# Three pairs of gate/up chunks in a SwiGLU feed-forward layer computed with tokens stationary and 512 weight columns moving

## The chip, the cores and the metric

The kernel runs on one core of a Trainium2 chip. The metric is the device time of one execution in microseconds (us). Five engines work side by side, each with its own instruction stream: TensorE (PE, with its weight loads as PEld), VectorE (DVE), ScalarE (ACT), GpSimd (POOL) and SyncE (SP, which here only issues DMAs). They wait for each other on semaphores. [...]

## What is computed

One layer of a hybrid encoder: three token mixers, a merge, an output projection, then a SwiGLU feed-forward part. The change is in the feed-forward part, with 512 tokens, D_MODEL = 1024 and D_FF = 2816, all in float32:

```
h2 = rms_norm(x, norm_ffn[l])
act = jax.nn.silu(jnp.einsum('bsd,df->bsf', h2, w_ffn_gate[l])) * jnp.einsum('bsd,df->bsf', h2, w_ffn_up[l])
x = x + jnp.einsum('bsf,fd->bsd', act, w_ffn_down[l])
```

## The kernel before

**Precision.** TensorE's fast float32 format (fp32r) keeps fewer bits than float32. So each operand is split into a high part (an ACT copy into fp32r) and a low part (a DVE subtraction, operand minus high part), and each product of blocks takes three matmuls: high by high, high by low, low by high. Weights are loaded by DMA as float32 and split on the chip, which costs one ACT and one DVE instruction per 128x1024 weight tile.

**Seven products for eight.** The 2816 columns of the gate and the up weight are taken in 11 chunks of 256. Chunks 0 and 1 are "direct" (`chan_chunk`, 128x512 matmuls). Chunks 2 to 10 use a 2x2 scheme of Strassen and Winograd (`seven`, L1543): the inner dimension 1024, the 512 tokens and the 256 columns are each halved, and of the eight block products only seven are computed, with sums of weight blocks (S1 to S4, `sums_a`, L1488, four DVE additions of 128x1024 per chunk) and differences of token blocks (T1 to T4, `diff_b`, L1454, computed once). Their order is `ORDER`: 11, 12, S2, S1, S3, S4, 22. A weight tile holds the block of the gate and that of the up weight side by side (128 partitions x 2 x 4 x 128).

**One product** (`product`, L310) is 24 matmuls: 128 weight columns are stationary, 256 token columns move, over 2 weights x 4 steps of the inner dimension x 3 parts. The result lies with channels on the partitions, as the down projection needs it. Partial results are copied out of PSUM by ACT (L1562) and the rest is added by DVE (L1536); `finish_act` (L1533) then applies Silu on ACT (L1537) and multiplies on DVE (L1538).

**Order of the work.** `make_a` (L1495) stays three products ahead of TensorE: it makes sums and splits (`split_a`, L1505: ACT at L1508, DVE at L1509) into tiles of three buffers. `load_a` (L1482) loads a chunk with eight SP DMAs of 256 KB, into a pool of eight tiles ("cor") one chunk ahead; the same eight tiles first hold the normalised tokens and T1 to T4 while `prepare_b` (L1458) splits them (DVE at L1451, sums at L1456). So a tile for weights comes free when DVE has read the token block in it. SP takes its DMAs strictly in order, so one whose tile is not free holds back all behind it. The order on each engine is otherwise set by a scheduler that follows the program's order. PSUM has four tiles of two banks ("mm", the pool `fp`).

**Elsewhere in the kernel** there are two stages of a form that the prediction needs. The q, k and v projections (L800 to L870) already use seven products with 128x512 matmuls (L844), an ACT copy (L857), a DVE addition (L865), a DVE transpose (L814), a store to DRAM by POOL and a load back. The down projection (L1602 to L1756) gets sums of its weights by accumulating POOL DMAs (L1629) onto tiles that SP loaded (L1626, L1641).

Of the kernel before, what the change touches and what calls it, by code (L numbers as in the profile page):

```python
# [16 lines left out]
P = 128  # L17
S = 512
D = 1024
# [3 lines left out]
NF = DFF // P  # L23
# [4 lines left out]
WARM = 9  # L28
GBUFS = 27
NDIRECT = 2  # L30
KD = 10
NTICK = (1, 1)
H = S // 2
# [29 lines left out]

@with_exitstack
def layer_kernel(ctx: ExitStack, tc: tile.TileContext, x, xt, vecs, w_in, w_qkv7, w_gate7, w_pool, w_rg, w_ig,
                 w_branch, w_br7, w_out, w_fg, w_fu, w_fd, w_fd7, out):
    nc = tc.nc
    act = nc.scalar.activation
    dve = nc.vector
# [3 lines left out]
    wp = ctx.enter_context(tc.tile_pool(name="wp", bufs=3))  # L73
# [4 lines left out]
    dr = ctx.enter_context(tc.tile_pool(name="dr", bufs=1, space=bass.MemoryType.DRAM))  # L78
# [12 lines left out]
    def cols(ap, k0, nk, c0, nc_):  # L91
        return ap[k0 * P:(k0 + nk) * P, c0:c0 + nc_].rearrange("(k p) c -> p k c", p=P)
# [217 lines left out]
    def product(a_, b_, ps, half, first, last, ws=(0, 1)):  # L310
        for w in ws:
            o = ps[:, w, half * H:(half + 1) * H]
            for k in range(4):
                for n, (a, b) in enumerate(((0, 0), (0, 1), (1, 0))):
                    nc.tensor.matmul(o, a_[a][:, w, k, :], il2(b_[b][:, k, :]),  # L315
                                     start=first and n == k == 0,
                                     stop=last and n == 2 and k == 3, skip_group_check=True)
# [119 lines left out]
    with ExitStack() as first:  # L437
# [411 lines left out]
        for t in VKQ:  # L849
            ps = {}  # L850
# [120 lines left out]
    with ExitStack() as mix:  # L971
# [299 lines left out]
        def corner(shape, name, dt=F32):  # L1271

            return cor.tile([P] + shape, dt, tag="r", name=name)
# [19 lines left out]
    with ExitStack() as third:  # L1293
# [42 lines left out]
        for u, nm in BORDER:  # L1336
# [5 lines left out]
            b = BH[nm]  # L1342
# [22 lines left out]
    with ExitStack() as ffn:  # L1365
# [85 lines left out]
            dve.tensor_tensor(l, BN[key], h.bitcast(F32), ALU.subtract)  # L1451
            B[which, nm] = h, l

        def diff_b(nm, x, y):  # L1454
            BN[nm] = corner([4, H], f"hn{nm}")
            dve.tensor_tensor(BN[nm], BN[x], BN[y], ALU.subtract)  # L1456

        def prepare_b():  # L1458
            nrm = [lambda k=k: norm2(k) for k in range(8)]
            return nrm[:4] + [lambda: split_b("11", (0, 0))] + nrm[4:] + [  # L1460
                lambda: split_b("21", (1, 0)),
                lambda: diff_b("T1", (0, 1), (0, 0)),
                lambda: diff_b("T2", (1, 1), "T1"),
                lambda: split_b("T2", "T2"),
                lambda: split_b("T1", "T1"),
                lambda: diff_b("T3", (1, 1), (0, 1)),
                lambda: split_b("T3", "T3"),
                lambda: split_b("22", (1, 1)),
                lambda: diff_b("T4", (1, 0), "T2"),
                lambda: split_b("T4", "T4")]  # L1470

        SUMS = {"S2": (("S3", "11", "21", ALU.subtract), ("S2", "22", "S3", ALU.subtract)),
                "S1": (("S1", "21", "22", ALU.add),),
                "S4": (("S4", "12", "S2", ALU.subtract),)}
# [5 lines left out]
        made = [0, NDIRECT]  # L1480

        def load_a(c):  # L1482
            for nm in ("11", "21", "22", "12"):
                raw[c, nm] = t = corner([2, 4, P], f"w{c}_{nm}")
                for w in range(2):
                    nc.sync.dma_start(t[:, w], cols((w_fg, w_fu)[w], KH[nm] * 4, 4, c * 256 + CH[nm] * P, P))

        def sums_a(c, nm):  # L1488
            for s_, x, y, op in SUMS.get(nm, ()):
                if (c, s_) in raw:  # L1490
                    continue
                raw[c, s_] = t = wp.tile([P, 2, 4, P], F32, tag="raw", name=f"w{c}_{s_}")
                dve.tensor_tensor(t, raw[c, x], raw[c, y], op)

        def make_a(upto):  # L1495
            while made[0] < min(upto, len(steps)):
                c, nm = steps[made[0]]
                made[0] += 1
                while made[1] < min(c + 2, DOWN):
                    load_a(made[1])  # L1500
                    made[1] += 1
                sums_a(c, nm)
                A[c, nm] = split_a(raw[c, nm], f"{c}_{nm}")

        def split_a(src, n):  # L1505
            h, l = (t.rearrange("p (w k c) -> p w k c", w=2, k=4)
                    for t in weight_tiles("wh" + n, "wl" + n))
            act(h, src, AF.Copy)  # L1508
            dve.tensor_tensor(l, src, h.bitcast(F32), ALU.subtract)  # L1509
            return h, l  # L1510

        acts = []
        DB = {}


# [17 lines left out]
        def finish_act(t, ps, a):  # L1533

            v = two2(t)
            dve.tensor_tensor(v, v, in_order2(ps), ALU.add)  # L1536
            act(t[:, 0, :], t[:, 0, :], AF.Silu)  # L1537
            dve.tensor_tensor(a, t[:, 0, :], t[:, 1, :], ALU.mult)  # L1538


        PRE = ("S2", "S1", "S3")
# [1 line left out]
        def seven(c):  # L1543
            a = g4([2, S], f"act{c}")
            tx, ty = g4([2, S], f"tx{c}"), g4([2, S], f"ty{c}")
            Y = fp.tile([P, 2, S], F32, tag="mm", name=f"ps_y{c}")
            X = fp.tile([P, 2, S], F32, tag="mm", name=f"ps_x{c}")
            lo, hi = slice(0, H), slice(H, S)
            plan = (("11", Y, 1, True, tx, lo, Y, hi),
                    ("12", X, 0, True, None, None, None, None),  # L1550
                    ("S2", Y, 1, False, tx, hi, Y, hi),
                    ("S1", X, 1, False, ty, hi, X, hi),
                    ("S3", Y, 1, False, ty, lo, Y, hi),
                    ("S4", X, 1, False, None, None, None, None),
                    ("22", Y, 0, False, None, None, None, None))
            n0 = steps.index((c, "11"))
            for n, (nm, ps, half, first, t, ts_, src, ss) in enumerate(plan):
                with tc.issue_after(last) if (c, n) == (NDIRECT, 3) else nullcontext():
                    make_a(n0 + n + 3)
                product(A.pop((c, nm)), B[0, WITH[nm]], ps, half, first, True)  # L1560
                if t is not None:
                    last = act(two2(t[:, :, ts_]), in_order2(src[:, :, ss]), AF.Copy).ins  # L1562
                if c == DOWN - 1 and nm in PRE:
                    split_d2("11", PRE.index(nm), 0, 0)
                if nm == "S4":
                    finish_act(tx, X, a[:, 0, :])
                if nm == "22":
                    finish_act(ty, Y, a[:, 1, :])
                if (c, n) in after:
                    after[c, n]()  # L1570
            acts.append(a)

        bg.extend([lambda: None, rms2] + prepare_b())
        for c in range(NDIRECT):
            pg = chan_chunk(("fg", c), h2, 3, fp)
            pu = chan_chunk(("fu", c), h2, 3, fp)
            if c == NDIRECT - 1:
                make_a(3)
            a = g4([2, S], f"act{c}")

            def direct_act(j, c=c, a=a, pg=pg, pu=pu):
                sg = small(f"sg{c}{j}", 2, "sq2")
                dve.tensor_tensor(two(sg), in_order(pg[j]), two(rb2), ALU.mult)
# [6 lines left out]
            acts.append(a)  # L1590
        tick(len(bg))
        after = {(NDIRECT, 1): lambda: direct_act(0), (NDIRECT, 2): lambda: direct_act(1)}
# [164 lines left out]


_INS = ["x", "xt", "vecs", "w_in", "w_qkv7", "w_gate7", "w_pool", "w_rg", "w_ig", "w_branch", "w_br7", "w_out",
        "w_ffn_gate", "w_ffn_up", "w_ffn_down", "w_down7"]  # L1760


# [41 lines left out]
```

## Time and profile before

| what | value |
|---|---|
| three timed runs | 859.97, 858.64, 859.10 us, median 859.1 |
| profiled execution, its own time | 858.89 us |
| its span in the trace | 856.8 us |
| direct gate/up matmuls end, chunk 2 begins | 580.5 us |
| chunks 2 to 7 | 580.5 to 693.2 us |
| chunks 8 to 10 | 693.2 to 749.5 us |

All positions are from the start of the span; 2.1 us lie around it. In the rows of the profile, `L315 PE` is an operation of TensorE issued at line 315, `out<-in` names the tiles, `xN` counts instructions, then come the busy time in us and the mean of one in ns, and behind the second bar the idle time of the engine ahead of them with what ended it. A DVE instruction's duration overlaps the next one's start by some 0.08 us, so a row's mean is a little longer than the distance between two starts.

### The profile page before, as it was taken

The page shows a single profiled execution, that of the slowest core. Times are in us where ns is not written, and L with a number is a line of the kernel's source. Part 1 is how long each engine was busy: PE and PEld are TensorE (multiplying, and loading weights), DVE is VectorE, ACT ScalarE, POOL GpSimd, SP SyncE. Part 2 cuts the span into 40 slices and gives each one's busy share as a digit, 9 for nine tenths or more (in the row PEclk, how much of TensorE's full clock was granted, in tenths as well). Part 3 has the DMA queues.
Part 4 walks back from the last instruction along what each step waited for, and adds up shares of the span by engine and source line. Part 5 has one row for each costly group of instructions (what it writes and reads, how often), then busy time and mean ns, then how long its engine had stood idle before and what let it go on. Part 6 is the DMA issues. An engine that isn't in the chain of part 4 may idle for free.

```text
span 856.8 us, 14307 instructions
## 1 busy us (share of the span) xinstructions
PE 850.3 (99%) x5483; PEld 781.2 (91%) x5483; DVE 732.3 (85%) x937; ACT 533.3 (62%) x863; POOL 88.6 (10%) x128
## 2 busy tenths in 40 slices
PE   9999999999999999999999999999999999999998
PEld 7888888888889988889889988889999999999998
DVE  7899898987897699967997877799988888999974
ACT  6554999658887657556665544455655555755642
POOL 1110002123324102000001100000000000121200
PEclk9999999999999999999999999999999999999999
DMA  9586356798585768846668854364533434797913
GB/s 343 160 286 205 101 167 200 215 316 262 141 257 129 228 170 239 246 116 171 174 204 212 182 197 148 99 164 136 145 99 109 114 101 142 221 238 204 199 32 123
DMA packets 141988, 154.09 MB, mean 180 GB/s; under 512 B 41696, under 2 KB 115424, under 8 KB 141920
## 3 DMA queue, kind: packets, MB, share of 16 engines
q1 hardware_dynamic: 129248, 107.30, 40.6%
q0 software_dynamic: 12528, 45.62, 22.5%
q8 instruction: 43, 0.70, 0.3%
q10 hardware_dynamic: 144, 0.26, 0.1%
q14 instruction: 25, 0.20, 0.1%
HBM read 132.71 MB, written 18.87 MB: 177 GB/s over the span
## 4 chain that ended last, share of the span: by engine, by line
PE 88%; ACT 4%; DVE 4%; issue 3%; POOL 1%; DMA 0%; DVEq 0%; POOLq 0%
PE ps_y L315 11%; PE ps_x L315 8%; PE ps_dy L1723 6%; PE ps_q L844 5%; PE ps_dx L1723 5%; PE ps_br L306 3%; PE ps_br L307 3%; PE ps_br L308 3%; PE ps_bY L1347 3%; PE ps_gy L315 3%; PE ps_gate L736 2%; PE ps_bX L1347 2%; PE ps_gx L315 2%; PE ps_pool L308 2%; PE ps_pool L306 2%
## 5 line engine op out<-in xcount | busy, mean ns | idle before, releaser
L141 ACT ACTIVATE whi<-raw 128x1024 fp32r<-128x1024 f32 x69 | 72.9, 1056 | 75.6 <-PE ps_br L307 18.4
L142 DVE TENSOR_TENSOR wlo<-raw,whi 128x1024 fp32r<-128x1024 f32 x69 | 84.2, 1220 | 22.4 <-ACT whi L141 21.9
L142 DVE TENSOR_TENSOR wlo<-qw,whi 128x1024 fp32r<-128x1024 f32 x48 | 58.3, 1220 | 11.6 <-ACT whi L141 11.2
L141 ACT ACTIVATE whi<-qw 128x1024 fp32r<-128x1024 f32 x48 | 50.4, 1052 | 23.6 <-PE ps_q L844 12.8
L1508 ACT ACTIVATE wh_S<-w_S 128x1024 fp32r<-128x1024 f32 x36 | 38.3, 1063 | 28.7 <-PE ps_y L315 20.0
L1629 POOL DMA_DIRECT2D dw<-in_w_down_dram x20 | 17.0, 855 | 305.3 <-DMA dw<-in_w_down_dram 247.7
L1509 DVE TENSOR_TENSOR wl_S<-w_S,wh_S 128x1024 fp32r<-128x1024 f32 x36 | 43.8, 1220 | 3.3 <-ACT wh_S L1508 3.3
L1508 ACT ACTIVATE wh<-w 128x1024 fp32r<-128x1024 f32 x27 | 28.6, 1061 | 28.0 <-PE ps_x L315 9.4
L1509 DVE TENSOR_TENSOR wl<-w,wh 128x1024 fp32r<-128x1024 f32 x27 | 32.9, 1220 | 8.2 <-ACT wh L1508 8.2
L1508 ACT ACTIVATE whdS<-dw 128x1024 fp32r<-128x1024 f32 x20 | 21.2, 1061 | 20.7 <-PE ps_dy L1723 10.6
L1155 DVE TENSOR_TENSOR_SCAN E<-K,ahead 128x512 f32<-128x512 f32 (+3 forms) x32 | 25.4, 814 | 4.6 <-ACT K L1151 4.6
L1509 DVE TENSOR_TENSOR wldS<-dw,whdS 128x1024 fp32r<-128x1024 f32 x20 | 24.3, 1221 | 5.2 <-ACT whdS L1508 5.2
L306 PE MATMUL ps_lru<-HH,whi 128*128 128x512 f32 x64 | 24.6, 384 | 0.0
L306 PE MATMUL ps_br<-yph,whi 128*128 128x512 f32 x64 | 24.4, 382 | 0.0
L306 PE MATMUL ps_gate<-HH,whi 128*128 128x512 f32 x64 | 24.4, 381 | 0.0
L307 PE MATMUL ps_br<-ypl,whi 128*128 128x512 f32 x64 | 24.3, 380 | 0.0
L306 PE MATMUL ps_pool<-HH,whi 128*128 128x512 f32 x64 | 24.3, 379 | 0.0
L306 PE MATMUL ps_br<-yHH,whi 128*128 128x512 f32 x64 | 24.3, 379 | 0.0
L307 PE MATMUL ps_lru<-HL,whi 128*128 128x512 f32 x64 | 24.3, 379 | 0.0
L308 PE MATMUL ps_lru<-HH,wlo 128*128 128x512 f32 x64 | 24.3, 379 | 0.0
L307 PE MATMUL ps_gate<-HL,whi 128*128 128x512 f32 x64 | 24.3, 379 | 0.0
L308 PE MATMUL ps_gate<-HH,wlo 128*128 128x512 f32 x64 | 24.3, 379 | 0.0
(742 smaller groups left out, 3432.1 us busy)
## 6 DMA issues: line engine op xcount, KB each, us to landing
raw<-in_w_in_dram SPq DMA_DIRECT2D x31, 512.0 KB, 5.1
qw<-in_w_qkv_dram SPq DMA_DIRECT2D x24, 512.0 KB, 7.2
dw<-in_w_down_dram POOLq DMA_DIRECT2D x20, 512.0 KB, 7.7
w<-in_w_ffn_gate_dram SPq DMA_DIRECT2D x36, 256.0 KB, 3.9
w<-in_w_ffn_up_dram SPq DMA_DIRECT2D x36, 256.0 KB, 4.1
raw<-in_w_branch_dram SPq DMA_DIRECT2D x16, 512.0 KB, 3.8
qw<-in_w_qkv_dram POOLq DMA_DIRECT2D x12, 512.0 KB, 7.6
g<-gd SPq DMA_DIRECT2D x24, 256.0 KB, 4.5
```

Source lines behind the costliest of these rows:

```text
L141: act(hi, raw, AF.Copy)
L142: los.append(dve.tensor_tensor(lo, raw, hi.bitcast(F32), ALU.subtract).ins)
L306: nc.tensor.matmul(ps, lh, rh, start=start, stop=False, skip_group_check=skip)
L307: nc.tensor.matmul(ps, lh, rl, start=False, stop=False, skip_group_check=skip)
L308: nc.tensor.matmul(ps, ll, rh, start=False, stop=stop, skip_group_check=skip)
L315: nc.tensor.matmul(o, a_[a][:, w, k, :], il2(b_[b][:, k, :]), start=first and n == k == 0, stop=last and n == 2 and k == 3, skip_group_che ...
L844: nc.tensor.matmul(ps[:, a, :], b_[:, k, ts_], il(a_[:, kk, :]), start=first and n == k == 0, stop=n == 2 and k == 3, skip_group_check=True)
L1155: dve.tensor_tensor_scan(E[:, c0:c0 + n][:, ::-1], K[:, c0 + 1:c0 + n + 1][:, ::-1], ahead[:, S - n:][:, ::-1], 0.0, ALU.mult, ALU.add)
L1347: nc.tensor.matmul(o, ah[x_][:, w, k, :], il2(b[k][y_]), start=first_ and n == k == 0, stop=n == 2 and k == 3, skip_group_check=True)
L1508: act(h, src, AF.Copy)
L1509: dve.tensor_tensor(l, src, h.bitcast(F32), ALU.subtract)
L1723: nc.tensor.matmul(o, a_[a][:, w, k0 + k, :], il2(b_[b][:, k, :]), start=first and i == k == 0, stop=last and i == 2 and k == nk - 1, skip ...
```

## The change

Chunks 2 to 7 become three units of two chunks (`NTOK = 3`, `seven_tok`). In a unit the roles of the operands are swapped: 128 tokens are stationary, 512 weight columns move. The same seven products are made, each in two half-steps (i = 0, 1) of 12 matmuls of 128x512. A half-step needs one weight tile of 128x1024, so a unit has 14 tiles to split, as two chunks have now. The results come with tokens on the partitions. ACT copies (`snap`) and DVE adds (`add`) them in tiles of 128x1024; `done` applies Silu, multiplies, transposes 32x32 blocks on DVE and stores to DRAM with POOL (two DMAs for each half of the unit); `load_act` brings each chunk back later with two SP DMAs. The rows of the down weight are permuted on the host to match what the block transpose leaves.

The weights of chunks 2 to 10 come from arrays packed on the host (`w_ffn7`, `w_ffnl7`), so that each load is one DMA of 512 KB with 4 KB in a row per partition. Sums of weights: in unit 0, S1 (21+22) and S3 (11+21) are made by accumulating POOL DMAs, S2 and S4 by DVE; in units 1 and 2, S1 is made so, S3 by adding 21 onto the tile of 11 with POOL, S2 and S4 again by DVE. Signs of T1, T2, T4 and of the sums are turned so that all sums of weights are additions; `diff_b` and `finish_act` use a scalar-tensor-tensor for the sign. Chunks 8 to 10 stay as they were, apart from their loads.

```diff
@@ weights
-        steps = [(c, nm) for c in range(NDIRECT, DOWN) for nm in ORDER]
+        NU = DOWN - NDIRECT - NTOK
+        steps = [(u, nm, i) for u in range(NU) for nm in ORDER for i in range(2 if u < NTOK else 1)]
...
+        def load_a(u):
+            if u >= NTOK:
+                for nm in ("11", "21", "22", "12"):
+                    raw[u, nm, 0] = t = corner([2, 4, P], f"w{u}_{nm}")
+                    nc.sync.dma_start(t, w_fgl7[u - NTOK, CH[nm], KH[nm]])
+                return
+            for nm, base, more in ((("21", "21", "22"), ("S3", "11", "21")) if u == 0
+                                   else (("11", "11", None), ("21", "21", "22"))):
+                for i in range(2):
+                    raw[u, nm, i] = t = corner([2, 512], f"w{u}_{nm}{i}")
+                    nc.sync.dma_start(t, usrc(u, base, i))
+                    if more:
+                        nc.gpsimd.dma_start(t, usrc(u, more, i), accum_op=ALU.add)
+
+        def load_raw(u, nm):
+            for i in range(2):
+                raw[u, nm, i] = t = (g4([2, 512], f"w{u}_{nm}{i}") if (u, nm, i) == (0, "12", 1) else
+                                     wp.tile([P, 2, 512], F32, tag="raw", name=f"w{u}_{nm}{i}"))
+                nc.sync.dma_start(t, usrc(u, nm, i))
+
+        def make_s2(u, i):
+            raw[u, "S2", i] = t = g4([2, 512], f"w{u}_S2{i}")
+            dve.tensor_tensor(t, raw[u, "21", i], raw[u, "11", i], ALU.add)
...
+                src = raw[u, nm if (u, nm) == (0, "S3") else FROM.get(nm, nm), i]
+                A[u, nm, i] = split_a(src, f"{u}_{nm}{i}", (2, 512))
...
+                if u and nm == "11":
+                    make_s2(u, i)
+                    nc.gpsimd.dma_start(raw[u, "11", i], usrc(u, "21", i), accum_op=ALU.add)
+                elif nm == "S2":
+                    dve.tensor_tensor(src, src, raw[u, "12", i], ALU.add)
+                    if i:
+                        load_raw(u, "22")
@@ one unit
+            def done(j):
+                g, t = v["g", j], v["u", j]
+                act(g, g, AF.Silu)
+                dve.scalar_tensor_tensor(t, t, -1.0, g, ALU.mult, ALU.mult)
+                dve.transpose(g.rearrange("p a c -> p (a c)"), t.rearrange("p a c -> p (a c)"))
+                for h in range(2):
+                    n = 4 * (2 * j + h)
+                    nc.gpsimd.dma_start(ad[u][:, n:n + 4].rearrange("m b (j i) -> (b j) m i", i=P),
+                                        g[:, h].rearrange("p (m i) -> p m i", i=P))
...
+                for i in range(2):
+                    make_a(n0 + 2 * n + i + 3)
+                    ah, al = A.pop((u, nm, i))
+                    for a in range(2):
+                        ts_ = slice(a * P, (a + 1) * P)
+                        for kk in range(2):
+                            k = 2 * i + kk
+                            for m, (b_, a_) in enumerate(((bh, ah), (bh, al), (bl, ah))):
+                                nc.tensor.matmul(ps[dst][:, a, :], b_[:, k, ts_], il(a_[:, kk, :]),
+                                                 start=dst == nm and m == k == 0, stop=m == 2 and k == 3,
+                                                 skip_group_check=True)
...
-        for c in range(NDIRECT, NF // 2):
-            if c == NF // 2 - 1:
+        for u in range(NTOK):
+            seven_tok(u)
+        for c in range(NDIRECT + 2 * NTOK, DOWN):
+            if c == DOWN - 1:
```

The loads of the first weights stand on SP's queue, behind the last loads of the direct chunks. Before, in SP's order, `w2_11` is block 11 of chunk 2, and each tile takes two DMAs:

```order
L1486 DMA w2_11_5787<-in_w_ffn_gate_dram 128x4x128
L1486 DMA w2_11_5787<-in_w_ffn_up_dram 128x4x128
L1486 DMA w2_21_5790<-in_w_ffn_gate_dram 128x4x128
L1486 DMA w2_21_5790<-in_w_ffn_up_dram 128x4x128
L1486 DMA w2_22_5793<-in_w_ffn_gate_dram 128x4x128
L1486 DMA w2_22_5793<-in_w_ffn_up_dram 128x4x128
L1486 DMA w2_12_5796<-in_w_ffn_gate_dram 128x4x128
L1486 DMA w2_12_5796<-in_w_ffn_up_dram 128x4x128
```

After, at the same place of SP's order; `w0_210` is block 21 of unit 0, half-step 0, and `w1_...` belongs to unit 1:

```order
L1509 DMA w0_110_5802<-in_w_ffn7_dram 128x1024
L1509 DMA w0_111_5804<-in_w_ffn7_dram 128x1024
L1501 DMA w0_210_5790<-in_w_ffn7_dram 128x1024
L1501 DMA w0_211_5793<-in_w_ffn7_dram 128x1024
L1501 DMA w0_S30_5796<-in_w_ffn7_dram 128x1024
L1501 DMA w0_S31_5799<-in_w_ffn7_dram 128x1024
L1509 DMA w0_120_5806<-in_w_ffn7_dram 128x1024
L1501 DMA w1_110_5903<-in_w_ffn7_dram 128x1024
L1501 DMA w1_111_5905<-in_w_ffn7_dram 128x1024
L1501 DMA w1_210_5907<-in_w_ffn7_dram 128x1024
L1509 DMA w0_121_5808<-in_w_ffn7_dram 128x1024
L1501 DMA w1_211_5910<-in_w_ffn7_dram 128x1024
```

The weights of the second product come after seven tiles (block 12 was fourth before); its second half, `w0_121`, has ten loads ahead of it, three of them for unit 1. On POOL, which issues no DMA there before, four accumulating DMAs go with them:

```order
L1503 DMA w0_210_5790<-in_w_ffn7_dram 128x1024
L1503 DMA w0_211_5793<-in_w_ffn7_dram 128x1024
L1503 DMA w0_S30_5796<-in_w_ffn7_dram 128x1024
L1503 DMA w0_S31_5799<-in_w_ffn7_dram 128x1024
L1503 DMA w1_210_5907<-in_w_ffn7_dram 128x1024
```

Each of them waits for the SP load of its tile. On DVE, before, from the low part of product 12 of chunk 2 on (`sg` and `act1` are the activation of direct chunk 1):

```order
L1509 TENSOR_TENSOR wl2_12_5816<-w2_12_5796,wh2_12_5815 128x1024
L1493 TENSOR_TENSOR w2_S3_5819<-w2_11_5787,w2_21_5790 128x1024
L1583 TENSOR_TENSOR sg10_5888<-ps_fg_1_5677,rb2_5160 128x512
L1493 TENSOR_TENSOR w2_S2_5821<-w2_22_5793,w2_S3_5819 128x1024
L1493 TENSOR_TENSOR w2_S1_5858<-w2_21_5790,w2_22_5793 128x1024
L1585 TENSOR_TENSOR sg10_5888<-sg10_5888,ps_fu_1_5738 128x512
L1509 TENSOR_TENSOR wl2_S2_5824<-w2_S2_5821,wh2_S2_5823 128x1024
```

And after, from the low part of the first half of product 12 of unit 0 on:

```order
L1553 TENSOR_TENSOR wl0_120_5819<-w0_120_5806,wh0_120_5818 128x1024
L1513 TENSOR_TENSOR w0_S20_5822<-w0_210_5790,w0_110_5802 128x1024
L1513 TENSOR_TENSOR w0_S21_5824<-w0_211_5793,w0_111_5804 128x1024
L1553 TENSOR_TENSOR wl0_121_5841<-w0_121_5808,wh0_121_5840 128x1024
L1717 TENSOR_TENSOR act1_5826<-sg10_5898,rb2_5160 128x512
L1717 TENSOR_TENSOR act1_5826<-sg11_5947,rb2_5160 128x512
L1553 TENSOR_TENSOR wl0_S20_5860<-w0_S20_5822,wh0_S20_5859 128x1024
L1542 TENSOR_TENSOR w0_S20_5822<-w0_S20_5822,w0_120_5806 128x1024
L1553 TENSOR_TENSOR wl0_S21_5877<-w0_S21_5824,wh0_S21_5876 128x1024
```

`wl0_121` stands ahead of the splits of S2, so while DVE waits for `w0_121`, these wait too.

More of the change, by code (lines that the diff above doesn't have):

```diff
@@ L30 @@
 NDIRECT = 2
+NTOK = 3
 KD = 10
@@ L1488, in sums_a, with usrc @@
[L1488 to L1493, printed above, removed]
+        made = [0, 0]
+        def usrc(u, nm, i):
+            return w_fgu7[u, CH[nm], KH[nm], i]
+        def load_a(u):
[11 more added lines that the diff above has]
+                        nc.gpsimd.dma_start(t, usrc(u, more, i), accum_op=ALU.add)
@@ L1496, in make_a @@
             while made[0] < min(upto, len(steps)):
-                c, nm = steps[made[0]]
+                u, nm, i = steps[made[0]]
                 made[0] += 1
-                while made[1] < min(c + 2, DOWN):
+                while made[1] < min(u + (1 if (u, nm) in ((0, "11"), (0, "12"), (0, "S2")) else 2), NU):
                     load_a(made[1])
                     made[1] += 1
[L1502 to L1507, printed above, removed]
+                if u >= NTOK:
+                    for s_, x, y, op in SUMS.get(nm, ()):
+                        raw[u, s_, 0] = t = wp.tile([P, 2, 4, P], F32, tag="raw", name=f"w{u}_{s_}")
+                        dve.tensor_tensor(t, raw[u, x, 0], raw[u, y, 0], op)
+                    A[u, nm, i] = split_a(raw[u, nm, 0], f"{u}_{nm}")
+                    continue
@@ L1510, in split_a @@
             return h, l
-        acts = []
+        acts = {}
         DB = {}
@@ L1555, in seven @@
                     ("22", Y, 0, False, None, None, None, None))
-            n0 = steps.index((c, "11"))
+            u = NTOK + c - (NDIRECT + 2 * NTOK)
+            n0 = steps.index((u, "11", 0))
             for n, (nm, ps, half, first, t, ts_, src, ss) in enumerate(plan):
-                with tc.issue_after(last) if (c, n) == (NDIRECT, 3) else nullcontext():
-                    make_a(n0 + n + 3)
-                product(A.pop((c, nm)), B[0, WITH[nm]], ps, half, first, True)
+                make_a(n0 + n + 3)
+                product(A.pop((u, nm, 0)), B[0, WITH[nm]], ps, half, first, True)
                 if t is not None:
@@ L1565, in seven @@
                 if nm == "S4":
-                    finish_act(tx, X, a[:, 0, :])
+                    finish_act(tx, X, a[:, 0, :], 1.0)
                 if nm == "22":
[L1568 to L1571, printed above, removed]
+                    finish_act(ty, Y, a[:, 1, :], -1.0)
+                if tail and nm in ("11", "S2"):
+                    tail.pop(0)()
+                if toload and nm in LOADS.get(u - NTOK, ()):
+                    with tc.issue_after(last):
+                        load_act()
@@ new lines, in seven, with load_act @@
+            acts[c] = a
+        ad = [dr.tile([4, S // 32, 4096], F32, tag=f"ad{u}", name=f"ad{u}") for u in range(NTOK)]
+        toload = []
+        tail = []
+        LOADS = {0: ("S4",), 1: ("S2",)}
+        def load_act():
+            c = toload.pop(0)
+            u, m = divmod(c - NDIRECT, 2)
+            acts[c] = t = g4([2, S], f"act{c}")
+            for w in range(2):
+                nc.sync.dma_start(t[:, w].rearrange("p (b i) -> p b i", i=32),
+                                  ad[u][2 * m + w].rearrange("b (p i) -> p b i", i=32))
@@ new lines, in seven_tok, with bank, snap, add @@
+        def seven_tok(u):
+            v = {}
+            def bank(n):
+                return fp.tile([P, 2, 512], F32, tag="mm", name=f"ps_{n}{u}")
+            def snap(key, ps):
+                v[key] = g4([2, 512], f"v{u}{key[0]}{key[1]}")
+                return act(two(v[key]), in_order(ps), AF.Copy).ins
+            def add(key, ps):
+                dve.tensor_tensor(two(v[key]), two(v[key]), in_order(ps), ALU.add)
+            def done(j):
[7 more added lines that the diff above has]
+                                        g[:, h].rearrange("p (m i) -> p m i", i=P))
+            def finish(j):
+                if u < NTOK - 1:
+                    done(j)
+                else:
+                    tail.append(lambda: done(j))
+            ps = {}
+            n0 = steps.index((u, "11", 0))
+            for n, nm in enumerate(ORDER):
+                dst = {"S2": "11", "S3": "11", "S4": "S1"}.get(nm, nm)
+                if dst == nm:
+                    ps[nm] = bank({"11": "yh", "12": "xl", "S1": "xh", "22": "yl"}[nm])
+                bh, bl = B[0, WITH[nm]]
+                for i in range(2):
[9 more added lines that the diff above has]
+                                                 skip_group_check=True)
+                if nm == "11":
+                    snap(("g", 0), ps["11"])
+                elif nm == "12":
+                    add(("g", 0), ps["12"])
+                elif nm == "S2":
+                    last = snap(("g", 1), ps["11"])
+                elif nm == "S1":
+                    snap(("u", 1), ps["S1"])
+                elif nm == "S3":
+                    last = snap(("u", 0), ps["11"])
+                    add(("u", 1), ps["11"])
+                elif nm == "S4":
+                    add(("g", 1), ps["S1"])
+                    finish(1)
+                else:
+                    add(("u", 0), ps["22"])
+                    finish(0)
+                if toload and nm in ("S2", "S3"):
+                    with tc.issue_after(last):
+                        load_act()
+                if (u, n) in after:
+                    after[u, n]()
+            toload.extend(range(NDIRECT + 2 * u, NDIRECT + 2 * u + 2))
```

64 lines of the change are left out of this document (42 added, 22 removed).

## The prediction

> **What bounds the kernel now.** I read the page's totals first, then the chain that ended last, then the waits of TensorE, then a table by stage. A difference under 0.2% (1.7 us) counts as no change, since a measurement of this kernel can tell no less. The page's span, busy shares and chain by engine:
>
> ```profile
> span 856.8 us, 14307 instructions
> PE 850.3 (99%) x5483; PEld 781.2 (91%) x5483; DVE 732.3 (85%) x937; ACT 533.3 (62%) x863; POOL 88.6 (10%) x128
> PE 88%; ACT 4%; DVE 4%; issue 3%; POOL 1%; DMA 0%; DVEq 0%; POOLq 0%
> ```
>
> TensorE is busy for all but 6.5 us and holds 88% of the chain; VectorE comes next with 85%. The waits of TensorE (us in total, times, longest):
>
> ```profile
> PE ps_q L844 <- DVE wlo L142: 1.5, 4, 0.5
> PE warm_ps L451 <- DVE warm L328: 1.1, 1, 1.1
> PE ps_gate L736 <- DVE lt L587: 0.4, 1, 0.4
> PE ps_q0S L844 <- DVE wlo L142: 0.2, 1, 0.2
> ```
>
> None is in the feed-forward part. The table by stretches has the busy time of PE, PEld, DVE, ACT and POOL, the granted clock, the share of the DMA engines and GB/s; chunks 2 to 7 are its third row:
>
> ```profile
> 10.00:14.00 4.00, 4.00 (x20) 3.51 (x19) 3.46 (x10) 3.58 (x6) 0.00 (x0) 1.00 1.05 399
> 560.00:580.50 20.50, 20.50 (x97) 17.95 (x97) 20.50 (x23) 12.44 (x13) 0.00 (x0) 1.00 0.76 201
> 580.50:693.20 112.70, 112.70 (x1010) 112.67 (x1010) 103.24 (x97) 64.31 (x80) 0.00 (x0) 1.00 0.44 122
> 757.50:774.00 16.50, 16.50 (x140) 16.23 (x139) 15.72 (x23) 8.71 (x11) 4.27 (x5) 1.00 1.07 215
> ```
>
> In this stage TensorE never stops, VectorE works 103 of 112.7 us, and the DMA engines are free for over half of it. So only fewer or quicker matmuls can shorten it, and only a late weight tile can lengthen it.
>
> **The matmuls.** The chain shows one product of the old form and a run of the new form's matmuls, from the q stage (start, us, count):
>
> ```profile
> 580.50 2.68 PE ps_y L315 x24
> 171.34 20.72 PE ps_q L844 x96
> ```
>
> A 256-column matmul takes 2.68/24 = 111.7 ns, a 512-column one 20.72/96 = 215.8 ns, which does the work of two. Six chunks are 6 x 7 x 2.68 = 112.6 us, and the stage's row says 112.7. Three units are 3 x 7 x 24 x 0.2158 = 108.8 us. The saving is **3.8 to 3.9 us**; I take 3.9. [...]
>
> **The work beside it.** The rows for one tile's work:
>
> ```profile
> L1508 ACT ACTIVATE wh<-w 128x1024 fp32r<-128x1024 f32 x27 | 28.6, 1061 | 28.0 <-PE ps_x L315 9.4 <-issue 9.3 <-PE ps_y L315 8.7
> L1509 DVE TENSOR_TENSOR wl<-w,wh 128x1024 fp32r<-128x1024 f32 x27 | 32.9, 1220 | 8.2 <-ACT wh L1508 8.2
> L1493 DVE TENSOR_TENSOR w_S<-w,w 128x1024 f32<-128x1024 f32 x18 | 22.0, 1223 | 0.5
> L857 ACT ACTIVATE r<-ps_q 128x1024 f32<-128x1024 f32 x9 | 9.2, 1021 | 4.1 <-DVE r L865 2.1 <-PE ps_q L844 2.1
> L865 DVE TENSOR_TENSOR r<-r,ps_q 128x1024 f32<-128x1024 f32 x9 | 10.9, 1208 | 0.2
> L814 DVE STREAM_TRANSPOSE sq<-r 128x1024 f32<-128x1024 f32 x8 | 9.9, 1241 | 0.5 <-ACT r L823 0.5
> L1660 DVE SCALAR_TENSOR_TENSOR act<-act,act 128x512 f32<-128x512 f32 x15 | 9.5, 685 | 0.0
> ```
>
> Per unit of 36.3 us (7 x 5.18), VectorE has 14 splits, 4 sums, 4 additions, 2 products of 128x1024 (twice 0.685, so 1.4 us each) and 2 transposes: 24 x 1.22 + 2.8, about 32 us; the overlap of neighbours takes some 2 us off. Before it had 36.4 us for two chunks of 37.5 (14 splits, 8 sums, 4 additions, 4 half-size products and waits, 103.24/3 = 34.4 with them). ACT has 14 x 1.06 + 4 x 1.02 + two Silus of 128x1024, about 21 us. Neither is the bound; their cover is 4 us and more in each unit. I add **0.2 us** for a late tile somewhere. The q stage bounds this from above: the same form with the same three buffers waited 1.5 + 0.2 = 1.7 us, in all of its units. The work on signs (`diff_b`, `finish_act`) keeps its number of instructions and stays under TensorE.
>
> The stores, loads back and accumulating DMAs of units 1 and 2 need their results a whole unit later, and a load back takes a few us, so I cost them at nothing; the DMA engines had 56% of the stage free. If that cover were gone, a tile of S3 would come late by one landing, priced below. Chunks 8 to 10 only get larger loads, and the down projection keeps its order.
>
> **The first unit.** Here cover is short. The first loads go into tiles that hold token blocks, until VectorE has read them. In the trace these are freed one by one (VectorE's timeline, start and duration; then SP's, the first loads of each tile before):
>
> ```profile
> 563.75 1.22 DVE L1456 TENSOR_TENSOR hnT<-hn,hnT 128x1024 f32<-128x1024 f32 x1
> 566.02 1.22 DVE L1456 TENSOR_TENSOR hnT<-hn,hnT 128x1024 f32<-128x1024 f32 x1
> 571.70 1.22 DVE L1451 TENSOR_TENSOR B022l<-hn,B022h 128x1024 fp32r<-128x1024 f32 x1
> ```
> ```profile
> 561.71 0.37 SPq L1486 DMA_DIRECT2D w<-in_w_ffn_gate_dram  x1
> 566.16 0.37 SPq L1486 DMA_DIRECT2D w<-in_w_ffn_gate_dram  x1
> 567.38 0.37 SPq L1486 DMA_DIRECT2D w<-in_w_ffn_gate_dram  x1
> 569.65 0.37 SPq L1486 DMA_DIRECT2D w<-in_w_ffn_gate_dram  x1
> 570.67 0.86 SPq L1486 DMA_DIRECT2D w<-in_w_ffn_gate_dram  x1
> ```
>
> After the change the same four releases let in `w0_210`, `w0_211`, `w0_S30`, `w0_S31`, and the next ones three tiles of unit 1; `w0_121` comes behind all of these. Beside them run four accumulating DMAs. Such a mix stands in the down projection before; the rows of three SP loads of 512 KB, issued at 747.4, 747.9 and 749.3 while POOL issued accumulations:
>
> ```profile
> L1626 SPq DMA_DIRECT2D dw<-in_w_down_dram x2: 383/383/383, 747.4 to 747.9; - x2
> DMA to landing us min/median/max: 6.1/7.8/9.4
> L1641 SPq DMA_DIRECT2D dr<-in_w_down_dram x1: 328/328/328, 749.3 to 749.3; - x1
> DMA to landing us min/median/max: 11.8/11.8/11.8
> 748.12 0.87 POOL L1629 DMA_DIRECT2D dw<-in_w_down_dram  x1 [14.85 <-DVE tx L1536]
> 750.38 0.86 POOL L1629 DMA_DIRECT2D dw<-in_w_down_dram  x1 [1.39 <-DVE act L1538]
> 752.42 0.84 POOL L1629 DMA_DIRECT2D dw<-in_w_down_dram  x1 [1.18 <-DVE wld L1509]
> ```
>
> They landed at 747.4 + 6.1 = 753.5, 747.9 + 9.4 = 757.3 and 749.3 + 11.8 = 761.1: one in 3.8 us, where 524 KB at 399 GB/s alone would take 1.3. So an accumulation costs a load 2.5 us. [...]
>
> Now the sum. `w0_211`, issued at 566.2, lands near 570 (3.9 us, the 256 KB loads of before):
>
> ```profile
> w<-in_w_ffn_gate_dram SPq DMA_DIRECT2D x36, 256.0 KB, 3.9
> ```
>
> Seven loads follow to `w0_121`. If four pay for an accumulation, it lands at 570 + 4 x 3.8 + 3 x 1.3 = 589.1; if one of the four is over by then, at 586.6. If an accumulation cost no more than a load, 570 + 11 x 1.3 = 584.3; if all seven loads paid, or all ran at the 215 GB/s of 757.5 to 774, 596.6 and 570 + 11 x 524 KB/215 = 596.8. I take 588.6, near the value by the count of accumulations. ACT (1.06) and VectorE (1.22) make it usable at 590.9. TensorE needs it after three half-steps of 12 x 0.2158 = 2.59 us: 580.5 + 7.8 = 588.3. The wait is **2.6 us**, from nothing (584.3 + 2.3 is before 588.3) to 10.6. VectorE is held by the same tile, and ACT by its copy just before; behind it on VectorE stand two products of the direct chunk (1.4 us) and the first split of S2 (1.2), usable at 593.5, as TensorE comes to it at 590.9 + 2.6 = 593.5. So the wait is paid once. The earlier `w0_120` lands third behind `w0_211`, at 570 + 11.4 = 581.4, and is needed at 585.7.
>
> Sum against the profiled execution: 858.9 - 3.9 + 2.6 + 0.2 = **857.8 us**. That execution (span 856.8 and 2.1 around it) was 0.2 us under the median of the three runs, 859.1; the forecast is 1.3 us under it, so no change that can be told.
>
> **The rivals.**
>
> (1) The loads keep up: accumulations slow them little, or they begin earlier. For it: 4 KB rows where the old loads had 512 B, and the DMA engines were busy for only 0.76 of 560 to 580.5. Against it: the 3.8 us spacing. The wait is 0 to 0.8 us: 858.9 - 3.9 + 0.2 + 0 to 0.8 = 855.2 to 856.0.
>
> (2) Slower: the wait lowers TensorE's clock. At the start, after idle, nine 512-column matmuls took 447 ns each:
>
> ```profile
> 1.06 4.02 PE L451 MATMUL warm_ps<-warm 128*128 128x512 bf16 x9 [1.06 <-DVE warm L328]
> ```
>
> If the wait for `w0_121` brought that rate back for one half-step, 12 x (447 - 216) = 2.8 us come on top; with the landing at 589.1 the wait is 3.1: 858.9 - 3.9 + 3.1 + 2.8 + 0.2 = 861.1. It decides from some wait over 1.1 us on, the longest in the rows at full clock; the longer the wait, the likelier. Against it: no stretch of the table shows a clock under 1.00, though no row says what 3 us do. [...]
>
> (3) Slower: all seven loads pay. Then the wait is 10.6 us and the time 858.9 - 3.9 + 10.6 + 0.2 = 865.8. Against it: only four accumulations are due by then.
>
> (4) The splits run late in steady state as in the q stage, 1.7 us beside the wait: 859.3. It is inside no change.
>
> **How the numbers follow.** My forecast with (4), 857.4 to 860.8: 0.42. Rival (1) and everything under 857.4, which takes a wait under 2.2 us: 0.41. Rivals (2) and (3): 0.13 and 0.04. So faster 0.41, same 0.42, slower 0.17. The range runs from 855.0 (no wait, nothing late) to 861.4, which is (2) with 0.3 us of (4); what is left out is (3), the worse part of (2) and a little below 855.0. The likeliest case's own range is 857.4 to 860.8.
>
> **What would show it.** Right: the seven products of a unit take 36.3 us of TensorE; TensorE shows one wait, at the second half of product 12 of unit 0, for the low part of `w0_121`, of 2 to 3 us, and its clock stays 1.00; the loads up to `w0_121` land 3 to 4 us apart while POOL accumulates. Wrong: no such wait (rival 1); a clock under 1.00 after it (rival 2); several waits of a few tenths in units 1 and 2 (4); or a wait of chunk 8 or of the down projection for a chunk loaded back from DRAM, which I cost at nothing.

## The result and the profile after

The changed kernel takes **864.38 us** (median of 4 runs, 863.22 to 865.31), the kernel before 858.87 us beside it (4 runs). The ratio is 1.0061, 95% interval 1.0043 to 1.0080: 5.5 us slower. The forecast was 857.8 us, no change, with a range of 855.0 to 861.4; the measured time lies above it.

The page of the changed kernel, its span, busy shares and chain by engine (profiled execution: 863.47 us):

```profile
span 861.7 us, 13247 instructions
PE 848.9 (99%) x4979; PEld 764.6 (89%) x4979; DVE 723.9 (84%) x925; ACT 530.3 (62%) x845; POOL 108.1 (13%) x152
PE 75%; issue 8%; DVE 7%; ACT 4%; DMA 4%; POOL 1%; SPq 0%; POOLq 0%; DVEq 0%; ACTq 0%
```

TensorE fell from 88% to 75% of the chain, and a DMA is on it with 4%, where there was none. TensorE's waits name the place:

```profile
PE ps_xl L1677 <- ACT wh L1552: 5.2, 1, 5.2
PE ps_q L845 <- DVE wlo L143: 1.5, 4, 0.5
PE warm_ps L452 <- DVE warm L329: 1.1, 1, 1.1
PE ps_xl L1677 <- DVE wl L1553: 0.5, 1, 0.5
```

The two waits of `ps_xl` are one event, the second half of product 12 of unit 0; everything else in the list was there before. The chain there (start, us, what):

```profile
573.43 18.98 DMA w<-in_w_ffn_dram
592.49 1.06 ACT wh L1552
593.58 1.24 DVE wl L1553
594.86 4.45 PE ps_xl L1677 x11
599.30 5.18 PE ps_yh L1677 x24
...
692.54 5.18 PE ps_yl L1677 x24
697.73 2.68 PE ps_y L316 x24
```

`w0_121` was issued at 573.43 and landed 19 us later. Behind it stand the two halves of the split, and then 11 matmuls that take 4.45 us where 2.4 would do. From there on every product takes 5.18 us, up to chunk 8 at 697.73, which began at 693.2 before. TensorE's timeline shows the gap and the slow matmuls singly:

```profile
588.00 0.38 PE L1677 MATMUL ps_xl<-wh,B021l 128*128 128x512 f32 x1
593.60 0.79 PE L1677 MATMUL ps_xl<-wh,B021h 128*128 128x512 f32 x1 [5.22 <-ACT wh L1552]
594.86 0.79 PE L1677 MATMUL ps_xl<-wl,B021h 128*128 128x512 f32 x1 [0.47 <-DVE wl L1553]
595.45 0.63 PE L1677 MATMUL ps_xl<-wh,B021l 128*128 128x512 f32 x1
...
598.43 0.44 PE L1677 MATMUL ps_xl<-wh,B021h 128*128 128x512 f32 x1
598.71 0.38 PE L1677 MATMUL ps_xl<-wl,B021h 128*128 128x512 f32 x1
```

And the stretches (busy time of PE, PEld, DVE, ACT and POOL, granted clock, DMA share, GB/s):

```profile
588.20:594.90 6.70, 1.01 (x3) 0.33 (x2) 1.32 (x2) 2.41 (x3) 1.48 (x2) 0.76 1.04 385
594.90:600.00 5.10, 5.10 (x15) 4.19 (x16) 5.07 (x6) 2.11 (x3) 0.22 (x1) 0.64 1.04 214
600.00:697.70 97.70, 97.70 (x455) 85.56 (x454) 79.85 (x70) 55.55 (x55) 11.30 (x14) 1.00 0.72 186
```

The balance by rows. Unit 0 begins at 580.45. Product S2 would begin four half-steps later, at 580.45 + 4 x 2.59 = 590.8; the row of its first matmul is at 599.14, so 8.3 us are lost, 6.4 in waiting (the low part's first matmul at 594.86 for 588.4) and 1.9 in the nine matmuls from there on, most of them 0.43 us apart. Without waits the stage takes 108.8 us, 3.9 less than before. So 8.3 - 3.9 = +4.4 of the +4.5 us at 697.73 is told; 0.4 more come after the last matmuls. That makes the 4.9 us between the two spans, 861.7 and 856.8. The times of the two profiled executions, 863.47 and 858.89, lie 4.6 us apart, since 1.8 us lie around the span here and 2.1 before. The profiled one is among the quicker two of its four runs (863.22 and 863.47; the others 865.29 and 865.31); what the other two lost beyond it stays open.

### The profile page after: what moved, and what is told of

Read it like the earlier page. It is cut to its first block, busy times and chain, and to the rows that moved or that the text cites. A ratio compares the mean times of both kernels' runs of the same rounds, so it can differ in the third digit from the quotient of the medians.

```text
span 861.7 us, 13247 instructions
## 1 busy us (share of the span) xinstructions
PE 848.9 (99%) x4979; PEld 764.6 (89%) x4979; DVE 723.9 (84%) x925; ACT 530.3 (62%) x845; POOL 108.1 (13%) x152
## 4 chain that ended last, share of the span: by engine, by line
PE 75%; issue 8%; DVE 7%; ACT 4%; DMA 4%; POOL 1%; SPq 0%; POOLq 0%; DVEq 0%; ACTq 0%
PE ps_dy L1856 6%; PE ps_q L845 5%; PE ps_dx L1856 5%; PE ps_yh L1677 5%; PE ps_y L316 4%; PE ps_xh L1677 4%; PE ps_br L308 3%; PE ps_br L309 3%; PE ps_br L307 3%; PE ps_x L316 3%; PE ps_bY L1348 2%; PE ps_gy L316 2%; PE ps_gate L737 2%; DMA w<-in_w_ffn_dram 2%; DVE wlo L143 2%
## 5 line engine op out<-in xcount | busy, mean ns | idle before, releaser
L1553 DVE TENSOR_TENSOR wl_S<-w_S,wh_S 128x1024 fp32r<-128x1024 f32 x26 | 31.6, 1220 | 11.9 <-ACT wh_S L1552 11.9
L1552 ACT ACTIVATE wh_S<-w_S 128x1024 fp32r<-128x1024 f32 x26 | 27.3, 1055 | 14.0 <-PE ps_y L316 6.9
L1552 ACT ACTIVATE whdS<-dw 128x1024 fp32r<-128x1024 f32 x20 | 21.2, 1058 | 21.3 <-PE ps_dy L1856 10.6
L308 PE MATMUL ps_br<-yHL,whi 128*128 128x512 f32 x64 | 24.4, 381 | 0.2 <-DMA yHL<-ydl 0.2
```

The source lines that it names most:

```text
L308: nc.tensor.matmul(ps, lh, rl, start=False, stop=False, skip_group_check=skip)
L1553: state["lo"] = dve.tensor_tensor(l, src, h.bitcast(F32), ALU.subtract).ins
```

## The experiments

Eight kernels ran, each timed beside the kernel before except the last. Two theories stood against each other: the one queue that SP's loads share, where `w0_121` has ten loads ahead and the accumulations slow it; or something in `w0_121`'s own place (its late tile) or in the accumulations alone. (In the order shown above, `w0_120` has six tiles ahead of it, not seven.)

**Unit 1's loads behind w0_121.** In `make_a`, with the DMA of `w0_121` kept in `state`, so that `issue_after` can queue others behind it:

```diff
-                    load_a(made[1])
+                    with tc.issue_after(state["ld", 0, "12", 1]) if made[1] == 1 else nullcontext():
+                        load_a(made[1])
```

> Only the order of loads on SP's queue changes: the three loads of unit 1 that stood ahead of w0_121 are queued behind it. Theory (one queue in order, a load and an accumulation together take 3.8 us): w0_121 lands one pair after w0_120, at 582.2 + 3.8 = 586.0 instead of 592.4, is usable at 588.3, and TensorE, which needs it at 588.2, waits 0.1 to 0.5 us at full clock. The 8.3 us lost there go down to 0.5 at most: 864.4 - 7.8 to 8.2 = 856.2 to 856.6 us. Rival (w0_121 is late by its own issue at 573.4 and by the accumulations, whatever stands ahead of it): the wait stays over 3 us, 859.5 us or more.

Measured: 855.42 us (854.56 to 856.18), ratio to before 0.9955 (0.9940 to 0.9969). SP issues `w0_120` at 570.5 and `w0_121` at 570.9; the two together:

```profile
L1509 SPq DMA_DIRECT2D w<-in_w_ffn_dram x2: 382/404/426, 570.5 to 570.9; - x2
DMA to landing us min/median/max: 11.7/13.4/15.1
```

They landed at 582.2 and 570.9 + 15.1 = 586.0, one pair apart and to the tenth where expected. In this run's waits of TensorE no line of the feed-forward part is left, so even the 0.1 us did not come: its unit 0 began at 580.8 and not at 580.45. The time is 0.8 us under the range expected, which was taken from the median 864.4; the 8.3 us were read from the profiled execution, which is 0.9 us quicker. The issue of `w0_121` came 2.5 us earlier by the new order and its landing 6.4 us earlier, so the issue alone doesn't explain it. The place of one load in a queue decides whether the change gains 3.9 us or loses 5.5.

**S3 of unit 0 behind it as well.** Only 21 is loaded ahead, and the loads and accumulations of S3 follow 12:

```diff
                         load_raw(u, "11")
                     load_raw(u, "12")
+                    if u == 0:
+                        with tc.issue_after(state["ld", 0, "12", 1]):
+                            load_a(-1)
```

> As the run before, and the two loads for S3 of unit 0 with their two accumulations are queued behind w0_121 too, so that two accumulations run before it and not four. Theory: w0_121, issued at 573.4, lands before 582, TensorE waits nowhere in unit 0, its clock stays 1.00, and the whole loss of 8.3 us goes: 856.1 us, 2.8 below the kernel before. Rival (S3, now later, is the next to be late; TensorE needs it at 601): a wait at product S3, 857 us or more.

Measured: 855.22 us (854.62 to 855.56), ratio 0.9950 (0.9934 to 0.9967). Its waits of TensorE are those of the kernel before, and its chain runs through the three units without a gap:

```profile
580.56 5.18 PE ps_yh L1683 x24
...
684.16 5.18 PE ps_yl L1683 x24
689.34 2.68 PE ps_y L316 x24
```

689.34 - 580.56 = 108.78 us for six chunks that took 112.7. `w0_121` was issued at 568.8, not at 573.4 as expected, and landed at 574.2. The time is 0.9 us under the 856.1 expected, and S3 did not become late. It is the fastest version seen, some 4 us under the kernel before; it and the run before it can't be told apart.

**The wait filled.** 24 matmuls on token blocks between the two halves of product 12:

```diff
+                    if (u, nm, i) == (0, "12", 1):
+                        ps["S1"] = bank("xh")
+                        for _ in range(24):
+                            nc.tensor.matmul(ps["S1"][:, 0, :], bh[:, 0, 0:P], bh[:, 0:2, :].rearrange("p k c -> p (k c)"),
+                                             start=True, stop=True, skip_group_check=True)
```

> Loads as in the changed kernel. 24 matmuls of 128x512 on token blocks are added between the two halves of product 12 of unit 0, into a bank that S1 overwrites later; they take 5.2 us in which TensorE waits now. Theory (idle time lowers the clock, and nine matmuls at 427 ns for 216 cost 1.9 us): the clock stays 1.00, w0_121 lands as late as before, the time is 864.4 - 1.9 = 862.5 us. Rival (the slow matmuls have another cause, such as the port on which weights are read late): they stay, 864.4 us.

Measured: 862.77 us (861.18 to 865.19), ratio 1.0042 (1.0026 to 1.0059). By the medians 1.6 us are back, but the runs overlap those of the changed kernel, so the size is read from the profile. The matmuls at the same place:

```profile
594.54 0.48 PE L1682 MATMUL ps_xl<-wl,B021h 128*128 128x512 f32 x1 [0.66 <-DVE wl L1553]
594.86 0.38 PE L1682 MATMUL ps_xl<-wh,B021l 128*128 128x512 f32 x1
...
602.80 0.48 PE L1682 MATMUL ps_xh<-wl_S,B0T1h 128*128 128x512 f32 x1 [0.22 <-DVE wl_S L1553]
```

`w0_121` is as late (usable at 594.5), the matmuls take 0.38 again, and the granted clock is 1.000 for 0.996. Product S2 begins 16.8 us after the unit's first matmul (597.02 - 580.26), where it was 18.7 (599.14 - 580.45): these are the 1.9 us. So the slow matmuls came from the idle time. The last line shows what is next: VectorE's queue, held up by the same tile, has the low part of S1 ready only at 602.8, 0.2 us late.

**No accumulation in unit 0.** 21 and 22 are loaded plainly, and VectorE makes S3 onto 11, S2, and S1 onto 21:

```diff
-            for nm, base, more in ((("21", "21", "22"), ("S3", "11", "21")) if u == 0
+            for nm, base, more in ((("21", "21", None), ("22", "22", None)) if u == 0
...
+                            dve.tensor_tensor(raw[u, "S3", j], raw[u, "11", j], raw[u, "21", j], ALU.add)
...
+                            dve.tensor_tensor(t, raw[u, "S3", j], raw[u, "22", j], ALU.add)
...
+                        dve.tensor_tensor(raw[u, "21", i], raw[u, "21", i], raw[u, "22", i], ALU.add)
```

> Unit 0 loads 21 and 22 plainly and VectorE makes S3, S2 and S1 (four more additions of 128x1024, 4.6 us of VectorE); no DMA accumulates before unit 1, and the loads of unit 1 stay ahead of w0_121. Theory (the accumulations take the time): the loads come 1.3 us apart, w0_121 lands at about 572 + 7 x 1.3 = 581, no wait there; VectorE may be late by up to 1 us for S2 or S1: 856.1 to 857.5 us. Rival (the three loads of unit 1 ahead of it are what counts, not the accumulations): a wait over 3 us stays, 859.5 us or more.

Measured: 859.48 us (857.98 to 860.93), ratio 1.0002 (0.9993 to 1.0011). On the loads the theory held, on VectorE it was too low. `w0_121`, issued at 573.2:

```profile
L1509 SPq DMA_DIRECT2D w<-in_w_ffn_dram x1: 699/699/699, 573.2 to 573.2; - x1
DMA to landing us min/median/max: 8.5/8.5/8.5
```

It landed at 581.7 for 581, with all of unit 1's loads still ahead and issued as late as in the changed kernel (573.4). So a late issue and the ten loads alone do no harm, nor do the accumulations without unit 1's loads (the first experiment); the two together do. But TensorE's waits moved, and the chain says why:

```profile
PE ps_yh L1682 <- ACT v0g L1646: 2.1, 1, 2.1
PE ps_yh L1682 <- DVE wl_S L1558: 1.2, 1, 1.2
```
```profile
588.55 1.22 DVE w_S L1540
589.77 1.13 DVE w L1547
590.91 2.27 DVE wl_S L1558 x2
593.18 2.27 DVE w_S L1545 x2
595.45 1.14 DVE w L1547
596.70 0.68 ACT wh_S L1557
597.67 1.04 ACT wh_S L1557
598.70 0.92 ACT v0g L1646
599.66 0.79 PE ps_yh L1682
```

VectorE's sums and splits run back to back to 596.6; the low part of S2 is late by 1.2 us behind them, and ACT's copy out of `ps_yh` stands behind the splits of S1, which wait for the last addition (L1547). Seven of the matmuls that follow are 0.43 us apart, and the granted clock is 0.51 from 599.6 to 603.1. From unit 0's first product at 580.29 to chunk 8 at 694.61 are 114.3 us for 108.8, so 5.5 us are lost, 3.3 of them in the two waits and some 1.8 in the slow matmuls. The four additions, 4.6 us of VectorE, and their place behind `w0_121` cost TensorE at least as much; that they are the cause rests on the chain alone.

**Plain copies in place of the accumulations.** In unit 0 the four DMAs lose their addition, so this kernel leaves out two of the sums of weights:

```diff
-                        nc.gpsimd.dma_start(t, usrc(u, more, i), accum_op=ALU.add)
+                        if u == 0:
+                            nc.gpsimd.dma_start(t, usrc(u, more, i))
```

> The four accumulating DMAs of unit 0 are replaced by plain DMAs of the same size from the same queue (the sums S1 and S3 of unit 0 are left out: 22 and 21 take their place); the order of the loads is that of the changed kernel. Theory (adding is what makes an accumulation dear): a load and a plain copy share the engines at 1.3 us each, 2.6 a pair, so from w0_S30 at 572 the next land near 575, 577, 580, 583, 584 and w0_121 at 585 to 586; no wait, 855.5 to 856 us. Rival (a second queue that takes turns with SP's costs this much whatever it carries): 3.8 us a pair, w0_121 at 592, 864 us.

Measured: 856.47 us (855.86 to 857.91), ratio 0.9969 (0.9955 to 0.9983). The chain has the load:

```profile
573.06 13.79 DMA w<-in_w_ffn_dram
```

It landed at 586.9, a little later than 585 to 586, and TensorE waited 0.2 + 0.8 us where no wait was expected, with the clock at 1.000; the time is 0.5 us above the range expected. From their issues and times to landing, the loads ahead landed at 576.7, 578.9, 581.5 and 584.0: 2.2 to 2.6 us a pair where accumulations make it 3.8. So the adding, not POOL's queue by itself, costs 1.2 us or more a pair (3.8 less 2.6).

**One load ahead, and two.** Only 11 of unit 1, first half (or both halves), stays ahead of `w0_121`:

```diff
-                    nc.sync.dma_start(t, usrc(u, base, i))
+                    with tc.issue_after(state["ld", 0, "12", 1]) if u == 1 and (nm, i) != ("11", 0) else nullcontext():
+                        nc.sync.dma_start(t, usrc(u, base, i))
```

> Of the three loads of unit 1 one stays ahead of w0_121, two go behind it. Theory: w0_121 lands one pair later than with none ahead, at 586.0 + 3.8 = 589.8; its high part is usable at 590.9 and its low part at 592.1, so TensorE idles 2.7 us and then 1 us more, 3.8 us in all: 855.3 + 3.8 = 859.1 us if such a gap leaves the clock at 1.00, and up to 1.9 more, 861.0, if it lowers it. Rival (position in the queue does not set the landing): as with none ahead, 855.3, or as with three, 864.

Measured: 860.11 us (858.40 to 861.25), ratio 1.0008 (0.9998 to 1.0017). The load and TensorE's timeline:

```profile
571.71 18.53 DMA w<-in_w_ffn_dram
```
```profile
591.43 0.48 PE L1678 MATMUL ps_xl<-wh,B021h 128*128 128x512 f32 x1 [2.50 <-ACT wh L1553]
592.69 0.48 PE L1678 MATMUL ps_xl<-wl,B021h 128*128 128x512 f32 x1 [0.78 <-DVE wl L1554]
593.01 0.38 PE L1678 MATMUL ps_xl<-wh,B021l 128*128 128x512 f32 x1
593.60 0.63 PE L1678 MATMUL ps_xl<-wl,B021h 128*128 128x512 f32 x1
...
596.58 0.43 PE L1678 MATMUL ps_xl<-wh,B021l 128*128 128x512 f32 x1
```

It landed at 590.2 (589.8 expected). The clock fell here too, after 2.5 and 0.8 us of idle time, and not at once: three matmuls still run fast. Of the ten runs the quickest, 858.40 us, has a granted clock of 1.000, the others 0.998 or 0.999 and 859.38 us or more; no trace of the quickest is kept, so that its wait was the same isn't shown. With two ahead:

> Two loads of unit 1 ahead of w0_121. Theory: the accumulations end at 590.1, so w0_121 lands at 591.1, 1.3 us before it does with three ahead; TensorE idles some 4 us before its high part and the clock falls; 862 to 863 us. Rival: as with three, 864.

One run gave 861.69 us. The load, issued at 571.99, landed at 589.7, 1.4 us before the time expected, and 0.7 us of that is that its unit 0 as a whole began that much earlier. From the landings and TensorE's timelines of the four kernels (us; the landing is counted from the first matmul of unit 0, the wait as in the balance above):

| loads of unit 1 ahead | landing of `w0_121` | wait | lost in slow matmuls | time |
|---|---|---|---|---|
| none | 5.2 | 0 | 0 | 855.4 |
| one | 9.2 | 3.7 | 1.8 | 860.1 |
| two | 9.9 | 4.4 | 2.8 | 861.7 (one run) |
| three | 12.0 | 6.4 | 1.9 | 864.4 |

The later in the queue, the later the landing and the longer the wait; the slow matmuls don't follow that order. The stretches in which the granted clock is down, with three, one and two loads ahead (the clock is third from the end of each row, and 0.99 or 1.00 on either side):

```profile
591.70:598.50 6.80, 4.43 (x10) 3.20 (x11) 4.88 (x6) 3.86 (x4) 1.68 (x2) 0.50 1.05 293
593.20:596.70 3.50, 3.50 (x10) 2.75 (x9) 3.47 (x5) 0.98 (x2) 1.70 (x2) 0.51 0.95 267
590.80:597.70 6.90, 6.38 (x14) 4.80 (x15) 6.41 (x7) 3.30 (x5) 1.70 (x2) 0.51 1.05 281
```

With three ahead 2.4 of the 6.8 us at half clock fell into TensorE's idle time and cost nothing; with two ahead nearly all of them were paid.

**Two units in place of three.** With the order of the fast version:

```diff
-NTOK = 3
+NTOK = 2
```

> The order of loads of the fast variant (S3 and unit 1 behind w0_121), and two units of two chunks in place of three, so five chunks stay in the old form. Theory (each unit saves 7 x (2 x 2.68 - 5.18) = 1.26 us of matmuls and nothing else): 855.2 + 1.3 = 856.5 us. Rival (the gain comes from the packed loads or from less work on VectorE, and not per unit): 855.2 us.

Measured: 856.75 us (856.00 to 858.59), ratio 0.9971 (0.9960 to 0.9983), against 0.9950 with three units. The intervals touch, so the profile says it better: two units run from 580.47 to 652.99, and the next chunk's old form follows at 2.68 us a product:

```profile
647.81 5.18 PE ps_yl L1683 x24
652.99 2.68 PE ps_y L316 x24
```

72.52 us for two units is 36.26 each, and two old chunks take 37.5, so each unit saves 1.26 us, as expected.

## Why the prediction was wrong

**The matmuls: right.** Three units take 108.8 us without waits, and 3.9 us are gained (108.78 in the second run).

**The work beside it: right.** No wait of TensorE in units 1 and 2, in chunks 8 to 10 or for a chunk loaded back; the 0.2 us for a late tile and rival (4) did not come. By the row from 600 on, VectorE works 79.85 of 97.70 us, 29.6 a unit, and ACT 20.6, as counted. (The 36.4 us given for VectorE before is not the sum of its parts, 26 x 1.22 + 4 x 0.685 = 34.5; nothing hangs on it.) The experiment without accumulations shows how thin the cover of unit 0 is: with four more additions on VectorE the kernel takes 4 us more than in the first experiment.

**The first unit: right place, wrong size.** The one wait is where it was put, for the tile it was put down to, though most of it is for the high part. The step that failed is the landing of `w0_121`, taken as 588.6; it was 592.4, and the wait was 6.4 us for 2.6. By the issues of the loads and their times to landing, `w0_211` landed at 569.9 (570 in the sum), `w0_S30` at 571.9, `w0_S31` at 578.4, then 582.2, 586.0, 589.9, 591.1 and 592.4. The accumulations landed at 578.5, 582.4, 586.2 and 590.1. So the price of a pair, 3.8 us, was right (a load and a plain copy from POOL take 2.2 to 2.6 us of it; the other 1.2 to 1.6 come with the adding), and so was the number of pairs, four, and 1.3 us each for the loads without one. What the sum had not is the 6.5 us from `w0_S30` to `w0_S31`, 2.7 more than a pair; the rest is 0.6 for `w0_S30` and 0.5 in the choice of 588.6 for 589.1. Without accumulations the same stretch took 3.2 us, 1.9 more than a load alone, and with plain copies 4.9, some 2.3 more than a pair. So most of this loss is there without accumulations. The DMA engines moved less in that stretch: in the run without accumulations they moved 271 GB/s in it and 397 after it, with busy shares of 0.86 and 1.00 (the last two numbers of the rows), though the load that ends it had been issued at 569.4:

```profile
571.80:575.00 3.20, 3.20 (x17) 2.80 (x16) 3.20 (x5) 2.53 (x5) 0.00 (x0) 1.00 0.86 271
575.00:580.00 5.00, 5.00 (x25) 4.38 (x24) 5.00 (x8) 1.04 (x1) 0.00 (x0) 1.00 1.00 397
```

Why they moved less stays open.

**The clock: the likeliest case had no term for it.** Rival (2) had a chance of 0.13 and a price of 2.8 us on a wait of 3.1. It did happen: 1.9 us on 6.4. The fill and the single load ahead show it as the result of idle time: with the gap filled the clock was 1.000, and after gaps of 2.5 and 0.8 us it was 0.51. The 1.1 us that the prediction took for the longest wait at full clock is the one ahead of the warm-up's nine slow matmuls, of 447 ns each (the granted clock reads 1.00 there); the longest ahead of matmuls at the full rate in those rows is 0.5. Rival (2) with the wait as it was, 858.9 - 3.9 + 6.4 + 1.9 = 863.3, comes within 0.2 us of the profiled execution's 863.47.

So the range was too narrow on the slow side for two reasons: 589.1 was taken as nearly certain, with every load at its price and no term for a stretch in which the loads themselves are slower, and the wait and the clock were priced as separate cases, though in these traces waits of one or two gaps of 0.8 us at most left the clock at 1.00, and every wait with a gap of 2.1 us or more lowered it. The bound of 10.6 us for the wait stood in the text and was given 0.04.

## What to carry to other kernels

When an edit saves time on the engine that is the bound, look at the first tiles of the new form before its steady state: here the steady state gave the 3.9 us as counted, and one load behind three that nobody needed yet took 8.3 away. Write down the landing of every load of the first products in queue order, with the pairs that share the engines (3.8 us each here), and queue whatever is not needed in the first products behind what is; a wait of some us on TensorE should then be priced with its slow matmuls as one term (here 1.8 to 2.8 us on waits of 3.7 to 6.4).

## What the runs showed of the hardware

- A 512 KB load and a 512 KB accumulating DMA that run together took 3.8 us (spacing of the landings in the changed kernel), a load and a plain copy 2.2 to 2.6 (plain copies), a load alone 1.2 to 1.3 (the last two in the changed kernel).
- Idle time on TensorE lowered its granted clock to 0.50 or 0.51: gaps of 5.2 and 0.5 us (changed kernel), 3.2 and 0.5 (two loads ahead), 2.5 and 0.8 (one ahead), and one of 2.1 us (without accumulations). The first matmul behind this last gap came 7.6 us after the first behind a gap of 1.2 us that had not lowered it. Gaps of 0.2 and 0.8 us (plain copies, clock 1.000) did not. The matmuls in the slow stretches were 0.43 us apart for 0.216, some seven to twelve of them.
- The slow stretch doesn't begin at a fixed distance from the gap: in the changed kernel the clock was down at 591.7, before the first matmul behind the gap (593.60); with one load ahead three matmuls after the gap ran at full rate, and it was down from 593.2 on. It lasted 3.5 us there and without accumulations, 6.8 and 6.9 us with three and two loads ahead.
